# Last head of a retention layer: another order of its output tiles, and its first-freed tiles in a pool of their own

## The chip, the core and the metric

The kernel runs on one core of a Trainium2 chip. A core has a matrix engine (TensorE, PE in the profile, with its weight loads as PEld), a vector engine (VectorE, DVE), an activation engine (ScalarE, ACT), a general engine (GpSimd, POOL) and a queue engine that mostly issues DMAs (SyncE, SP). They run at the same time and wait for each other through semaphores; each works off its own instructions in the order in which they were placed. Operands lie in SBUF (128 partitions), matmul results in PSUM, eight banks of 128 x 512 fp32.

The metric is the time of one execution in microseconds of device time. A profiled execution gives the trace; its times are counted from the start of its span.

## The reference

One inference step of a two-layer decoder, on 512 prompt tokens and 32 sample tokens (8 sequences of 4) with shared weights. In what follows the 544 columns T are these tokens, prompt first.

```python
for i in range(DEPTH):            # layer 0: gated short convolution, layer 1: retention
    x = x + mixer(rmsnorm(x, norm_mix[i]))
    x = x + swiglu(rmsnorm(x, norm_ffn[i]))      # d_ff 2816
return rmsnorm(x, final_norm), conv states, retention states

def retention_mixer(x, s0, pos, w_in, gn_g, w_out):      # 4 heads, dk 256, dv 512
    q, k, v, g = split(x @ w_in)
    q, k = rotary(q, pos), rotary(k, pos) / 16
    o, S = retention_chunkwise(q, k, v, s0)      # decayed scores @ v + q @ state
    o = (o - mean(o)) * rsqrt(var(o) + 1e-6) * gn_g      # per head
    return (silu(g) * o) @ w_out, S
```

The sample tokens read and update a state of 256 x 512 per head and sequence; the prompt's state is an output. Everything is fp32.

## The kernel before

**Products.** Each fp32 operand is split into a high part (rounded, written by ScalarE) and a low part (the difference, by VectorE): `split`, L187. A product is three matmuls: high-high, high-low, low-high (`project`, L165, for 272 columns at a time; `mm3`, L160). The features lie on partitions, so `x` is 8 tiles of 128 x 544. Weights come by DMA into three rotating buffers `w` and are split into three rotating pairs `wh`, `wl`, all of one pool for the whole kernel. For three output-projection weight tiles of the last head the low part comes from ScalarE and a DMA that adds (`split_adding`, L192).

**Stages.** Convolution layer, first feed-forward, retention layer, second feed-forward, final norm. Each feed-forward (`ffn`, L545) works in 2 x 2 blocks with seven products in place of eight: VectorE and ScalarE form sums of weight blocks (`weights7`, L424) and of activation blocks (`operands_left`, `operands_rest`, L403 and L408). `run` (L511) goes through 22 jobs, gate and up by turns; a job's products come in the order 1, 5, 6, 2, 7, 4, 3 for the first one, and the weights of the next are prepared ahead. `gate` (L591) applies Silu. Product 1 and 5 need only the first four `x` tiles, the others all eight.

**Retention, head by head** (L1166). Values and keys; gate tiles 0 to 3 (`gate_project`, L994: matmuls, times the norm's factor, Silu, gain); scores; then the output by token tiles of 128: `inner(h, st, it)` (L1042), 9 matmuls of 512 columns for tile 2, 12 for tile 3; `sample_outputs` (L1100) and `states_update` (L1113) for the four parts of the samples' state, whose load (`states_load`, L1095) takes the buffer that an earlier part's store frees. `normalized` (L1030) takes mean and variance on VectorE, the power on POOL, and scales. `gated` (L1059) transposes a normalized tile on TensorE (4 transposes) and multiplies it with the gate on VectorE. `out_project` (L1132) splits the gated tiles (`yh`, `yl`) and adds eight output tiles to `x`, two to each weight tile, in the order 0, 1, 4, 5, 2, 3, 6, 7. The last head has no next head's work to overlap, so its gate tiles 2 and 3 are kept back to cover its waits, and the first weight tile's two outputs are done by halves of 272 columns: the first half needs token tiles 0, 1 and a part of 2, the second the rest.

**What sets the order.** A planner goes through the program once with estimated durations. On each engine it places next the instruction that comes first in the program among those that it reckons to be ready; a later one can fill a gap. So an instruction's place in the program is its rank, not its time. `issue_after` pins an instruction behind another. The engines then run that fixed order, and wait where the estimate was too early.

**Memory.** Pools lie in SBUF as a stack, in the order in which they are opened; a stage's pools take the addresses of the stage before, and a tile waits for the old tiles that it covers. In the retention layer the stack is `vp` (17.4 KB to a partition: values, later `yh` and `yl`), `tp` (tiles in the order of first use: `gt`, `rot0`, `rot1`, `rt0`, `rt1`, the split keys and queries, ...), `one`, `sp` (three state buffers). The second feed-forward stacks its gate and up tiles (17.4 KB) and then `sw` (18.4 KB), where the sums of weight blocks are made and split. So `sw` covers `gt`, `rot0`, `rot1`, `rt0`, `rt1` and a part of the keys. In the last head `gt` and `rot1` hold normalized tiles (L1216, L1224) and `rot0` one part of the prompt's mid state.

**PSUM.** Two double banks (`psum()`) and four single banks (`bank()`).

## Time and profile before

| | us |
|---|---|
| median of three runs (lowest, highest) | 1467.85 (1467.62, 1469.62) |
| the profiled execution | 1468.62 |
| its span, first to last instruction | 1466.4 |
| TensorE busy | 1449.5 (99%) |
| VectorE, ScalarE, POOL busy | 959.4, 632.1, 130.5 |
| DMA | 189.62 MB, mean 129 GB/s |

In the trace the last head's gate tiles 2 and 3 run from 1031.6 to 1046.2 us, its first output matmul stands at 1052.8, the last at 1080.0, and the second feed-forward's first product follows at 1080.1.

How to read the rows. A row of the timeline gives start, duration, engine, line, instruction, output<-inputs, a count where equal rows were merged, and in brackets the idle time before it and what ended it. Durations of neighbours on one engine overlap by some 0.1 us, so that start to start is shorter. A row of the windows gives, for a stretch, the busy time of each engine with the number of instructions, the TensorE clock granted (1.00 is full), the DMA share and GB/s. A row of the waits names who waited for whom. Tile names have lost their numbers: `h` and `l` are the split weight sums, `oh` and `ol` the split activation blocks, `f` the blocks before the split.

### The profile page before, as it was taken

How to read it: one execution, taken by the hardware profiler on the slowest of the kernel's cores; microseconds unless marked ns; L12 is line 12 of the kernel's file. 1: busy time of each engine (PE TensorE's matmuls, PEld its weight loads, DVE VectorE, ACT ScalarE, POOL GpSimd, SP SyncE). 2: the span in 40 equal slices, each digit the busy share in tenths (PEclk: the TensorE clock that was granted, in tenths of full speed). 3: DMA queues.
4: the chain of work that ended last, by engine and by line, in shares of the span. 5: the costliest groups of instructions: out<-in, count | busy, mean ns of one | idle time of the engine just before them, and what ended most of it. 6: DMA issues, size and time to landing. Idle time of an engine off the chain costs nothing.

```text
span 1466.4 us, 26224 instructions
## 1 busy us (share of the span) xinstructions
PE 1449.5 (99%) x10920; PEld 1378.7 (94%) x10920; DVE 959.4 (65%) x1489; ACT 632.1 (43%) x925; POOL 130.5 (9%) x171
## 2 busy tenths in 40 slices
PE   9999999999999999999999999999999999999997
PEld 9999999999999999898988978987789999999997
DVE  5644678848748557648546835835698847748655
ACT  5222467626536435241141223214286626526434
POOL 0100011101101003000000000000111101101002
PEclk9999999999999999999999999999999999999999
DMA  6222246635536436237234623713646635536432
GB/s 225 78 95 89 89 104 146 153 109 130 130 108 149 125 73 199 92 115 258 75 124 164 202 81 112 253 53 120 202 113 140 146 115 129 143 106 140 122 80 83
DMA packets 80694, 189.62 MB, mean 129 GB/s; under 512 B 7728, under 2 KB 25008, under 8 KB 80576
## 3 DMA queue, kind: packets, MB, share of 16 engines
q1 hardware_dynamic: 66576, 162.01, 35.2%
q0 software_dynamic: 13136, 24.72, 10.3%
q8 instruction: 85, 1.39, 0.4%
q10 hardware_dynamic: 864, 1.22, 0.2%
q14 instruction: 33, 0.27, 0.1%
HBM read 166.75 MB, written 21.18 MB: 128 GB/s over the span
## 4 chain that ended last, share of the span: by engine, by line
PE 90%; DVE 6%; DMA 1%; ACT 1%; POOL 1%; issue 1%; DVEq 0%; POOLq 0%; ACTq 0%
PE mm L173 37%; PE sm L476 31%; PE sm L173 8%; PE sm L897 2%; PE sm L898 2%; PE sm L899 2%; PE sm L161 1%; PE sm L163 1%; PE sm L162 1%; PE sm L1108 1%; DVE S L1129 1%; DMA w<-in_ffgu_dram 1%; DVE ol L189 1%; DVE wl L189 1%; DMA S<-in_rets_dram 1%
## 5 line engine op out<-in xcount | busy, mean ns | idle before, releaser
L188 ACT ACTIVATE wh<-w 128x1024 fp32r<-128x1024 f32 (+4 forms) x139 | 129.6, 936 | 346.6 <-PE mm L173 223.3
L476 PE MATMUL sm<-oh,wh 128*128 128x272 f32 x704 | 204.2, 290 | 3.1 <-ACT oh L188 1.7
L476 PE MATMUL sm<-ol,wh 128*128 128x272 f32 x704 | 203.5, 289 | 1.1 <-DVE ol L189 1.1
L476 PE MATMUL sm<-oh,wl 128*128 128x272 f32 x704 | 203.3, 289 | 0.2 <-DVE wl L420 0.2
L173 PE MATMUL mm<-xh,wh 128*128 128x272 f32 x932 | 195.3, 290 | 0.0
L173 PE MATMUL mm<-xh,wl 128*128 128x272 f32 x932 | 192.5, 289 | 0.0
L173 PE MATMUL mm<-xl,wh 128*128 128x272 f32 x932 | 192.4, 288 | 0.0
L189 DVE TENSOR_TENSOR wl<-w,wh 128x1024 fp32r<-128x1024 f32 (+4 forms) x139 | 150.2, 1085 | 27.7 <-ACT wh L188 25.4
L269 DVE TENSOR_TENSOR x<-x,mm 128x544 f32<-128x544 f32 x91 | 65.4, 719 | 139.1 <-PE mm L173 139.0
L476 PE MATMUL sm<-oh,h 128*128 128x272 f32 x528 | 152.0, 288 | 0.0
L476 PE MATMUL sm<-oh,l 128*128 128x272 f32 x528 | 151.7, 288 | 0.0
L476 PE MATMUL sm<-ol,h 128*128 128x272 f32 x528 | 151.6, 287 | 0.0
L173 PEld LDWEIGHTS mm<-xh,wh 128*128 128x128 f32 x932 | 146.5, 189 | 4.8 <-DVE wl L189 3.4
L173 PEld LDWEIGHTS mm<-xl,wh 128*128 128x128 f32 x932 | 146.2, 189 | 0.1
L173 PEld LDWEIGHTS mm<-xh,wl 128*128 128x128 f32 x932 | 145.5, 189 | 0.2
L476 PEld LDWEIGHTS sm<-oh,wh 128*128 128x128 f32 x704 | 132.7, 188 | 4.6 <-ACT oh L188 2.3
L476 PEld LDWEIGHTS sm<-ol,wh 128*128 128x128 f32 x704 | 132.8, 189 | 1.5 <-DVE ol L189 1.5
L476 PEld LDWEIGHTS sm<-oh,wl 128*128 128x128 f32 x704 | 133.5, 190 | 0.5 <-DVE wl L420 0.5
L422 POOL DMA_DIRECT2D wl<-in_ffgu_dram x88 | 75.5, 858 | 647.9 <-ACT wl L421 298.3
L419 ACT ACTIVATE wh<-w 128x1024 fp32r<-128x1024 f32 x88 | 93.3, 1060 | 75.0 <-PE sm L476 47.9
L476 PEld LDWEIGHTS sm<-oh,h 128*128 128x128 f32 x528 | 99.4, 188 | 0.2 <-ACT oh L188 0.2
L476 PEld LDWEIGHTS sm<-oh,l 128*128 128x128 f32 x528 | 99.6, 189 | 0.0
(260 smaller groups left out, 3087.3 us busy)
## 6 DMA issues: line engine op xcount, KB each, us to landing
w<-in_ffgu_dram SPq DMA_DIRECT2D x88, 512.0 KB, 4.0
wl<-in_ffgu_dram POOLq DMA_DIRECT2D x88, 256.0 KB, 4.7
w<-in_ffdn_dram SPq DMA_DIRECT2D x96, 192.0 KB, 2.6
S<-in_rets_dram SPq DMA_DIRECT2D x16, 1024.0 KB, 7.6
out_rets_dram<-S SPq DMA_DIRECT2D x16, 1024.0 KB, 5.5
w<-in_cvin_dram SPq DMA_DIRECT2D x21, 512.0 KB, 3.5
w<-in_rtqk_dram SPq DMA_DIRECT2D x16, 512.0 KB, 3.6
w<-in_rtv_dram SPq DMA_DIRECT2D x16, 512.0 KB, 3.6
```

Of the source, the lines that this page charges most:

```text
L161: nc.tensor.matmul(out, lh, rh, start=start, stop=False, skip_group_check=True)
L162: nc.tensor.matmul(out, lh, rl, start=False, stop=False, skip_group_check=True)
L173: last_product[0] = nc.tensor.matmul(half(pt, hf)[:, :HT], w[:, c], act[k][:, hf * HT : (hf + 1) * HT], start=(first and k == ks[0] and i ...
L188: h = nc.scalar.activation(dh, src, AF.Copy)
L189: last_low[0] = nc.vector.tensor_sub(dl, src, dh.bitcast(F32))
L269: last_residual[0] = nc.vector.tensor_add(xk, xk, p)
L419: nc.scalar.activation(wh, w, AF.Copy)
L422: nc.gpsimd.dma_start(wl[:, n:], src[:, n:], accum_op=ALU.add)
L476: last = nc.tensor.matmul(out, w[:, c], b[k][:, at, :], start=(first and k == 0 and i == 0), stop=(k == n - 1 and i == 2), skip_group_chec ...
L897: nc.tensor.matmul(out, xh[kt][:, ts_], wh[:, cw], start=(kt == 0), stop=False)
L898: nc.tensor.matmul(out, xh[kt][:, ts_], wl[:, cw], start=False, stop=False)
L899: nc.tensor.matmul(out, xl[kt][:, ts_], wh[:, cw], start=False, stop=(kt == KT - 1))
```

## The change

Five edits; the numbers of matmuls stay, as do the shapes, but for three output tiles.

1. The one-element activation at the start that makes ScalarE load a function table is a Silu, not a Copy.
2. The last head's order: token tile 2's `inner` moves from ahead of gate tiles 2 and 3 to behind them, next to tile 3's. The normalized rows of tile 2 and of the samples go into a state buffer (`free`), not into `gt` and `rot1`.
3. `out_project` of the last head does output tiles 0, 1 and 4 by parts: the first 256 columns (token tiles 0 and 1) for all three, then `rest()`, which transposes and gates the samples, tile 2 and tile 3, then the other 288 columns. Each part is added to `x` by itself. The third tile's parts lie in two single banks.
4. `gt`, `rot1`, `rt1` and the split keys move to a pool `ep` between `vp` and `tp`, 19.1 KB to a partition, which is where the feed-forward's `sw` comes to lie.
5. The first job's weights are prepared (`jobs[0].prepare()`) before the activation blocks are made, no longer after.

```diff
-                nc.scalar.activation(warm, ones[:, 0:1], AF.Copy)
+                nc.scalar.activation(warm, ones[:, 0:1], AF.Silu)
...
     def run(jobs, after, steps):
 
         jobs[0].lead = True
-        jobs[0].prepare()
         jobs[0].begin()
...
             wide("m")
+            jobs = [job for m in range(HJ) for job in gate_up(m)]
+            jobs[0].prepare()
             made = None
             for kt in PAIRED[layer]:
                 made = operand(kt)
...
         vp = c2.enter_context(tc.tile_pool(name="rtv", bufs=1, reuse_waits="tile"))
+
+        ep = c2.enter_context(tc.tile_pool(name="rte", bufs=1, reuse_waits="tile"))
         tp = c2.enter_context(tc.tile_pool(name="rt", bufs=2, reuse_waits="tile"))
...
-            gt = tp.tile([P, 2, T], F32, tag="gt", name=nm("gt"), bufs=1)
+            gt = ep.tile([P, 2, T], F32, tag="gt", name=nm("gt"), bufs=1)
...
-                tp.tile([P, 2, T], F32, tag=f"rot{w}", name=nm("rot"), bufs=1) for w in range(2)
+                pool.tile([P, 2, T], F32, tag=f"rot{w}", name=nm("rot"), bufs=1) for w, pool in enumerate((tp, ep))
...
-            t1 = tp.tile([P, T], F32, tag="rt1", name=nm("rt1"), bufs=1)
+            t1 = ep.tile([P, T], F32, tag="rt1", name=nm("rt1"), bufs=1)
...
+            pool = ep if which else tp
+            th = pool.tile([P, 2, SEQ], F32R, tag=f"qkh{which}", name=nm("qkh"), bufs=1)
+            tl = pool.tile([P, 2, SEQ], F32R, tag=f"qkl{which}", name=nm("qkl"), bufs=1)
...
-        def normalized(src, tag="yn"):
+        def normalized(src, yn=None):
...
-            split_gated(slice(0, HT if rest else T))
-            wide("m" if rest else "mms")
-            for n2 in (0, 2, 1, 3):
-                wh, wl = load_piece(a["rtout"][h, n2], 2 * 4 * P, adding=rest is not None and n2 > 0)
-                pts = []
-                for n in range(2):
-                    pts.append(psum())
-                    if n2 == 0 and rest:
-                        rest[n]()
-                        project(pts[n], wh, wl, n * 4 * P, yh, yl, hfs=(0,))
-                    else:
-                        project(pts[n], wh, wl, n * 4 * P, yh, yl)
-                        residual(2 * n2 + n, pts[n])
-                if n2 == 0 and rest:
-                    split_gated(slice(HT, T))
-                    for n in range(2):
-                        project(pts[n], wh, wl, n * 4 * P, yh, yl, hfs=(1,))
-                        residual(n, pts[n])
+            cut = 2 * P
+            def part(pt, w, n, c):
+
+                for k in range(4):
+                    at = slice((n % 2 * 4 + k) * P, (n % 2 * 4 + k + 1) * P)
+                    mm3(
+                        pt[:, : c.stop - c.start], w[0][:, at], w[1][:, at], yh[k][:, c], yl[k][:, c], k == 0, k == 3
+                    )
+
+            order = (0, 1, 4, 5, 2, 3, 6, 7)
+            ws, parts = {}, {}
+            split_gated(slice(0, cut if rest else T))
+            wide("m" if rest else "mms")
+            for i, n in enumerate(order):
+                if i % 2 == 0:
+                    ws[n // 2] = load_piece(a["rtout"][h, n // 2], 2 * 4 * P, adding=rest is not None and n > 0)
+                if rest and i < 3:
+                    parts[n] = psum() if i < 2 else [bank(), bank()]
+                    part(half(parts[n], 0), ws[n // 2], n, slice(0, cut))
+                    if i == 2:
+                        rest()
+                        split_gated(slice(cut, T))
+                        for m, pt in parts.items():
+                            part(half(pt, 1), ws[m // 2], m, slice(cut, T))
+                            for c, b in ((slice(0, cut), 0), (slice(cut, T), 1)):
+                                nc.vector.tensor_add(x[m][:, c], x[m][:, c], half(pt, b)[:, : c.stop - c.start])
+                    continue
+                pt = psum()
+                project(pt, *ws[n // 2], n % 2 * 4 * P, yh, yl)
+                residual(n, pt)
...
             sample_outputs(h, st, 2)
-            p2 = inner(h, st, 2)
             if more:
+                p2 = inner(h, st, 2)
                 nxt = qk_start(h + 1)
...
             else:
-                yn2 = normalized(p2, "gt")
                 gate_project(h, st, 2, lambda: states_update(h, st, 2))
...
                 gate_project(h, st, 3, inside)
-                yns = normalized(st["po"], "rot1")
                 gated_pair(h, st, (yn0, 0), (yn1, 1))
-                gated(h, st, yn2, 2)
-                p3 = inner(h, st, 3)
-                gated(h, st, yns, 4)
+                p2, p3 = inner(h, st, 2), inner(h, st, 3)
+                free = sp.tile([P, 4, DV], F32, tag="S", name=nm("yn"))
+                yns, yn2 = normalized(st["po"], free[:, 0, :]), normalized(p2, free[:, 1, :])
                 yn3 = normalized(p3)
-                out_project(h, st, [lambda: None, lambda: gated(h, st, yn3, 3)])
+
+                def rest():
+                    gated(h, st, yns, 4)
+                    gated(h, st, yn2, 2)
+                    gated(h, st, yn3, 3)
+
+                out_project(h, st, rest)
```

The tiles `v4` (tag `rot1`) and one of `v2` (tag `rt1`) move to `ep` with their tags, in the same way.

10 lines of the change are left out of this document (4 added, 6 removed).

## The prediction

> **What bounds the kernel.** I read the page's busy shares first, then who TensorE waited for, then single stretches. The page:
>
> ```profile
> PE 1449.5 (99%) x10920; PEld 1378.7 (94%) x10920; DVE 959.4 (65%) x1489; ACT 632.1 (43%) x925; POOL 130.5 (9%) x171
> ```
>
> TensorE is busy 99% of the span and no matmul is removed, so only its waits and its slow stretches can be won. All its waits from 1046 to 1100 us (the last head and the start of the second feed-forward), then two from the list for the whole span (columns: us in total, times, longest):
>
> ```profile
> PE sm L476 <- ACT oh L188: 1.7, 1, 1.7
> PE mm L173 <- ACT yh L188: 1.2, 1, 1.2
> PE sm L476 <- DVE ol L189: 0.8, 1, 0.8
> PE sm L161 <- DVE yn L1039: 0.4, 1, 0.4
> PE sm L1063 <- DVE yn L1039: 0.3, 1, 0.3
> PE sm L476 <- ACT g L536: 0.2, 1, 0.2
> PE sm L476 <- DVE wl L420: 0.2, 1, 0.2
> ...
> PE sm L476 <- ACT u L536: 0.8, 1, 0.8
> ...
> PE sm L173 <- DVE rs L222: 0.3, 1, 0.3
> ```
>
> Three sit at the feed-forward's start (oh 1.7, ol 0.8, wl 0.2: 2.7 us), four in the last head. Busy time by stretch (PE, PEld, DVE, ACT, POOL with instruction counts; PEclk; DMA):
>
> ```profile
> 1058.70:1080.10 21.40, 21.40 (x170) 21.17 (x170) 20.50 (x38) 19.39 (x31) 1.73 (x2) 1.00 0.31 62
> ...
> 1051.00:1054.40 3.40, 2.11 (x14) 1.47 (x12) 2.89 (x8) 1.39 (x4) 0.73 (x1) 1.00 0.80 155
> 1054.40:1057.80 3.40, 3.22 (x15) 3.22 (x16) 1.43 (x5) 0.00 (x0) 0.00 (x0) 0.52 0.20 39
> ...
> 1081.70:1085.10 3.40, 0.84 (x4) 0.41 (x4) 3.40 (x8) 2.11 (x4) 0.00 (x0) 1.00 0.00 0
> 1085.10:1088.50 3.40, 3.18 (x13) 2.91 (x14) 3.40 (x6) 1.72 (x4) 0.85 (x1) 0.53 0.46 118
> ...
> 1065.00:1088.70 23.70, 20.80 (x150) 19.88 (x149) 23.41 (x42) 20.73 (x33) 2.59 (x3) 0.93 0.33 72
> ```
>
> A 272-column matmul takes 21.40/170 = 0.126 us. A stretch in which TensorE idled is twice followed by 3.4 us at a granted clock of 0.52 and 0.53: half of 3.22 and of 3.18 us, 1.6 us lost each time. So the losses that the change can touch are: 0.8 (L536, in the first feed-forward) + 0.3 (gate tile 2) + 0.4 + 1.2 + 0.3 (output projection's start) + 1.6 + 2.7 + 1.6 + 0.2 = **9.1 us**. From 1065 on VectorE is busy 23.41 of 23.70 us: it, not TensorE, sets when the last operands of the second feed-forward exist.
>
> **The change, part by part.**
>
> *Silu in the warm-up.*
>
> ```profile
> 221.41 1.28 ACT L598 ACT_TABLE_LOAD   x1
> ...
> 225.34 0.38 ACT L536 ACTIVATE u<-sm 128x272 f32<-128x272 f32 x1
> ...
> 225.77 0.39 PE L476 MATMUL sm<-oh,wh 128*128 128x272 f32 x1 [0.84 <-ACT u L536]
> ```
>
> The load in front of the first Silu goes; the one at the warm-up stays, in time that waits for the first DMA anyway. ScalarE's queue behind it comes 1.28 us earlier, more than the 0.84 that TensorE waited for the snapshot. Bounds 0 and 0.8; I take 0.8, as ScalarE ran without a gap from the load to that snapshot.
>
> *Output tile 2 moved behind the gate tiles.* Its nine 512-column matmuls change place, not number. Its PSUM bank is no longer held while gate tile 2 asks for two, so that wait (0.3) goes. Both gate tiles come earlier by 0.3 and by the nine matmuls; but with them comes the last state's product (L1108), which needs a state from memory:
>
> ```profile
> 1050.11 0.40 PE L162 MATMUL sm<-vl,sh 128*128 128x512 f32 x1
> 1050.34 0.39 PE L163 MATMUL sm<-vh,sl 128*128 128x512 f32 x1
> ...
> 1031.91 1.51 SPq L1098 DMA_DIRECT2D S<-in_rets_dram  x1
> ...
> S<-in_rets_dram SPq DMA_DIRECT2D x1, 1024.0 KB, 8.6
> ...
> 1041.72 1.04 PE L1108 MATMUL sm<-S,qm 128*8 128x512 f32 x8
> ...
> 800.46 1.05 PE L1108 MATMUL sm<-S,qm 128*8 128x512 f32 x8 [0.24 <-DMA S<-in_rets_dram]
> ```
>
> Nine matmuls of 0.23 are 2.1 us, so the product is reached at 1041.72 - 2.4 = 1039.3, while the state lands at 1031.91 + 8.6 = 1040.5. Nothing moves the load: SP issues it behind the second state's store, as before. That is a new wait of 1.2 us; head 1 shows the same wait, 0.24, at a margin that the planner had thought enough. Bounds 0 (the planner puts the rest of gate tile 3 in front) and 1.2; I take 1.2, by the load's own row. Behind it on TensorE stand the last state update and half of gate tile 3, whose end I call E: 1046.2 - 2.4 + 1.2 = 1045.0.
>
> *From E to the first output matmul.*
>
> ```profile
> 1047.55 0.78 DVE L1006 TENSOR_TENSOR gate<-sm,R 128x272 f32<-128x272 f32 x2
> 1049.84 0.69 DVE L1066 TENSOR_TENSOR gate<-gate,mm 128x512 f32<-128x512 f32 x1 [1.51 <-ACT gate L1008]
> 1051.04 0.69 DVE L1035 BATCH_NORM_STATS2 bst<-sm 128x6 f32<-128x512 f32 x1
> 1053.71 0.81 DVE L1039 TENSOR_SCALAR yn<-sm,mv,rs 128x512 f32<-128x512 f32 x1 [0.46 <-POOL rs L223]
> ```
>
> From the gate's first multiplication to the end of the pair's gating is 1051.0 - 1047.55 = 3.5 us (two rows of 0.6 net each at its end). After E that is E + 0.4 + 3.5, and the first split is done near E + 4.4. TensorE has meanwhile 8 transposes (0.9), tile 2 (2.1) and tile 3 (12 x 0.23 = 2.8): until E + 5.8. The 1.2 and the 0.4 are covered. What is late next is tile 3's normalization: 1054.5 - 1051.0 = 3.5 us on VectorE and POOL, so E + 5.8 + 0.3 + 3.5 = E + 9.6. The three 256-column parts (36 x 0.126 x 256/272 = 4.3 us) cover it to E + 10.1. The 0.3 goes too, with half a microsecond to spare. The tile that now holds the normalized rows takes the second state's buffer, whose store is issued ahead of the load at 1031.91: free long before E.
>
> *The end of `rest`.* Its 12 transposes (1.3 us) now stand together, and nothing else on TensorE is ready behind them: all further output matmuls need the 288 columns that are gated and split last.
>
> ```profile
> 1057.55 0.69 DVE L1066 TENSOR_TENSOR gate<-gate,sm 128x512 f32<-128x512 f32 x1 [1.97 <-PE sm L1063]
> 1058.27 1.39 ACT L188 ACTIVATE yh<-gate 128x272 fp32r<-128x272 f32 x4 [4.53 <-DVE gate L1066]
> ...
> 1058.75 0.52 PE L173 MATMUL mm<-yh,wh 128*128 128x272 f32 x2
> ```
>
> Last transpose to gating, split and matmul took 1.2 us there, under other matmuls; in the new order it lies open. Bounds 0 (the planner puts the transposes among the parts) and 1.2; I take 1.2. With it may come a half-clock stretch as after 1051-1054.4, where PE's rows cover 2.11 of 3.40 us: bounds 0 and 1.6; the new gap is as long as the old one, but how it falls into the clock's stretches isn't known, so I take 0.8. The second parts, 36 x 0.133 = 4.8 us, and five whole tiles, 120 x 0.126 = 15.1, then run without a gap: T + 19.9, T being their start, E + 12.6.
>
> *Weights first, in memory that is free early.* The rows of the first job's weights on VectorE:
>
> ```profile
> 1047.28 0.35 SPq L431 DMA_DIRECT2D w<-in_ffgu_dram  x1
> ...
> 1060.14 0.68 DVE L434 TENSOR_TENSOR w<-w 128x512 f32<-128x512 f32 x1
> ...
> 1085.03 0.68 DVE L420 TENSOR_TENSOR wl<-w,wh 128x512 fp32r<-128x512 f32 x1
> 1085.64 1.00 DVE L189 TENSOR_TENSOR ol<-f,oh 128x816 fp32r<-128x816 f32 x1
> ...
> 1086.91 1.21 DVE L189 TENSOR_TENSOR l<-w,h 128x1024 fp32r<-128x1024 f32 x1
> 1088.04 0.72 DVE L189 TENSOR_TENSOR ol<-f,oh 128x544 fp32r<-128x544 f32 x1
> ```
>
> Four sums (L434 to L437, 0.6 net each: 2.4) and two low parts (1.1 + 0.6) no longer need memory that the normalized tiles hold, and the later of the two loads that they read is issued at 1047.28: 4.1 us can go into VectorE's gap from E + 9.6 to E + 11.6 and the smaller gaps about it. What remains after T: 23.41 - 1.7 (L420, L189 `l`) = 21.7 us of operands, sums of squares and residuals, 1.7 of the same that ran before 1065, two L420 (1.2), and 0.3 for the residuals in two pieces: 24.9. From the first residual at T + 1.9, less the last square (0.6), the last operand stands at T + 26.2. TensorE can do products 1 and 5 and the first three blocks of one or two more without it, 33 to 42 matmuls: to T + 24.1 or 25.2. Stall 1.0 to 2.1; I take 1.5, and no half clock, in place of 2.7 + 1.6. Bounds: 0, and 5.6 if the 4.1 us stay where they are. The second job's weights follow the operands on ScalarE and VectorE and are needed 60 matmuls (7.6 us) after T + 19.9: in time, barely. SP's order of loads is untouched; POOL gets the same three powers, later. The 0.2 at L536 stays.
>
> **Sum.** 9.1 lost before; after 1.2 + 1.2 + 0.8 + 1.5 + 0.2 = 4.9; gain 4.2 us. The profiled execution took 1468.62 us (span 1466.4 and 2.2 around it) and would take 1464.4; it stands 0.8 above the median of the runs, 1467.85, so the forecast is **1463.6 us**.
>
> **Rivals.**
> - *No half clock.* The remaining idle pieces are too short: 0.8 less, 1462.8. For it: none of the new gaps is longer than 1.5 us. Against it: the gap of 1.2 before 1054.4 was enough. The Trainium skill ("TensorE: Matmul & The Clock Gate", Part 1) says that the clock halves after an idle window of about 3.4 us, and its closing table warns of gaps over some 3 us; by that rule this rival holds. The trace disagrees: 1.2 us of waiting, with PE's rows covering 2.11 of 3.40 us, was followed by a clock of 0.52.
> - *VectorE stays the bound.* The sums and low parts find no gap before T: 4.1 us come back, 1467.7, no change that can be told. For it: VectorE was idle before 1057.55 with L434's load landed, and L434 still came at 1060.14. Against: its memory was then the normalized tiles'.
> - *Slower: ScalarE blocks on the weights.* Now written ahead of the operands, `weights7`'s first rounding (L419) needs the `wh` buffer that the second output weight tile gives back when output tiles 4 and 5 are done, T + 4.8 + 3.0 = T + 7.8. If it stands in ScalarE's queue ahead of the first operand scaling (L580), ready at T + 2.0, all operands slip 5.8 us, and the longer stall adds a half-clock stretch, 1.6: 1463.6 + 7.4 = 1471.0. It decides as soon as L419 precedes the third L580. Against it, the rows of before, where it was placed at the buffer's release:
>
> ```profile
> 1061.66 0.75 ACT L580 ACTIVATE f<-x,vec 128x544 f32<-128x544 f32 x1 [2.01 <-DVE x L269]
> ...
> 1069.02 1.05 ACT L419 ACTIVATE wh<-w 128x1024 fp32r<-128x1024 f32 x1
> ```
>
> **How the numbers follow.** The measurement tells 0.2%, 2.9 us, from no change. Forecast 0.52, its own range 1459.2 (all goes but the 0.2 and one small wait) to 1464.9; no half clock 0.12; VectorE the bound 0.20; ScalarE blocked 0.12; 0.04 for an order that the planner changes elsewhere, on the slow side. Faster 0.64, within 0.2% 0.20, slower 0.16. The range takes in all but the outer part of the blocked case: 1459.0 to 1470.5.
>
> **What would show it.** Right: one table load; no wait of gate tile 2; L1108 of the last head waiting about 1 us for its state; no gap before the first `yh` matmul; one gap of about 1.2 after the last transposes; L434 before T; the wait for `oh` and `ol` at L476 under 2 us. Wrong: L434 still after the splits, L419 ahead of the L580s, two half-clock stretches, or a new wait over 1 us anywhere between 230 and 1030 us.

## The result, and the profile after

The changed kernel takes 1473.2 us (median; 1472.22 to 1473.75) against 1467.85 for the kernel before, measured beside it: a ratio of 1.0032, with a 95% interval of 1.0021 to 1.0044. It is slower by some 5 us, where 4.2 us of gain were forecast. The profiled execution has a span of 1470.3 us, 3.9 more than before. The page of the changed kernel, busy times:

```profile
PE 1450.5 (99%) x10920; PEld 1379.5 (94%) x10920; DVE 959.7 (65%) x1492; ACT 631.3 (43%) x924; POOL 130.9 (9%) x171
```

The work is the same; only waits and slow stretches can differ. Where TensorE waited in the changed kernel between 1032 and 1102 us (total, times, longest):

```profile
PE mm L161 <- ACT yh L188: 2.6, 2, 1.4
PE sm L476 <- ACT oh L188: 1.6, 2, 1.3
PE sm L476 <- DVE wl L420: 1.3, 1, 1.3
PE sm L476 <- DVE ol L189: 1.1, 2, 0.7
PE sm L1112 <- DMA S<-in_rets_dram: 0.5, 1, 0.5
PE mm L162 <- DVE yl L189: 0.2, 1, 0.2
```

The last head's waits (`yh`, S, `yl`) sum to 3.3 us and those at the feed-forward's start (`oh`, `wl`, `ol`) to 4.0, where before had 2.7. The same kernel by stretches of 3.41 us (busy time of PE, PEld, DVE, ACT, POOL; clock granted to TensorE; DMA):

```profile
1083.46:1086.87 3.41, 1.46 (x8) 1.01 (x8) 3.41 (x8) 3.41 (x7) 0.00 (x0) 0.99 0.00 0
1086.87:1090.28 3.41, 3.41 (x15) 3.41 (x15) 3.41 (x7) 1.65 (x3) 0.85 (x1) 0.51 0.35 40
1090.28:1093.70 3.42, 1.66 (x10) 1.15 (x9) 3.42 (x5) 2.90 (x4) 0.47 (x1) 0.99 0.24 42
1093.70:1097.11 3.41, 3.41 (x17) 3.41 (x17) 1.70 (x4) 0.00 (x0) 0.39 (x1) 0.50 0.87 215
1097.11:1100.52 3.41, 3.41 (x18) 3.41 (x17) 1.71 (x4) 0.79 (x2) 1.57 (x1) 0.51 0.52 169
```

Three of the five stretches have the clock at half: 5.1 us lost (half of 10.24), where before had one such stretch at this place (1.7 us). Two follow directly on a stretch with 1.8 to 2.0 us of waits. The third follows a stretch in which TensorE did not wait at all; what that stretch holds comes up below.

The last head's output ends 0.4 us earlier than before (first matmul of the feed-forward behind it: 1079.7 against 1080.1). The spread of the norm's factor, L227, comes at 1102.22 against 1098.28, 3.9 us later, and this is the whole difference of the spans. So, on balance, everything is lost in the 22 us in which the second feed-forward starts.

What VectorE did there (start, duration, idle time before in brackets):

```profile
1061.93 0.79 DVE L1172 TENSOR_TENSOR x<-x,mm 128x256 f32<-128x256 f32 x2 [0.71 <-PE mm L163]
1063.39 0.79 DVE L1172 TENSOR_TENSOR x<-x,mm 128x256 f32<-128x256 f32 x2 [0.67 <-PE mm L163]
...
1064.85 0.45 DVE L1172 TENSOR_TENSOR x<-x,sm 128x288 f32<-128x288 f32 x1 [0.32 <-PE sm L163]
1066.53 0.73 DVE L189 TENSOR_TENSOR ol<-f,oh 128x544 fp32r<-128x544 f32 x1 [1.22 <-ACT oh L188]
...
1070.23 0.68 DVE L434 TENSOR_TENSOR w<-w 128x512 f32<-128x512 f32 x1
...
1088.96 0.68 DVE L435 TENSOR_TENSOR w<-w,w 128x512 f32<-128x512 f32 x1
1089.57 0.68 DVE L436 TENSOR_TENSOR w<-w,w 128x512 f32<-128x512 f32 x1
1090.17 0.71 DVE L189 TENSOR_TENSOR ol<-f,oh 128x544 fp32r<-128x544 f32 x1
```

It stood still for 2.9 us at the beginning, and L434, L435 and L436 in these rows are sums for the *second* job: the first job's were done by 1059 us. The last operand's low part, `ol`, comes at 1090.17 (before: 1088.04). ScalarE, in the same kernel:

```profile
1063.41 1.05 ACT L194 ACTIVATE wh<-w 128x1024 fp32r<-128x1024 f32 x1
...
1064.91 1.04 ACT L195 ACTIVATE wl<-wh 128x1024 fp32r<-128x1024 f32 x1
1065.86 0.64 ACT L188 ACTIVATE oh<-f 128x544 fp32r<-128x544 f32 x1
...
1067.61 1.06 ACT L419 ACTIVATE wh<-w 128x1024 fp32r<-128x1024 f32 x1
...
1090.32 1.06 ACT L419 ACTIVATE wh<-w 128x1024 fp32r<-128x1024 f32 x1
1091.36 1.06 ACT L188 ACTIVATE h<-w 128x1024 fp32r<-128x1024 f32 x1
1092.32 0.61 ACT L421 ACTIVATE wl<-wh 128x512 fp32r<-128x512 f32 x1
1092.84 0.38 ACT L535 ACTIVATE g<-sm 128x272 f32<-128x272 f32 x1
```

The first job's weights (L419 at 1067.61) stand among the operands, and from 1090.32 three roundings for the second job stand in front of the first job's own snapshot (L535). In before the snapshot came ahead of all of them:

```profile
1088.44 0.40 ACT L536 ACTIVATE g<-sm 128x272 f32<-128x272 f32 x1 [0.22 <-PE sm L476]
```

The loads of the second job's weights, of which L430 is issued first and L431 second, in before and then in the changed kernel:

```profile
1063.39 0.35 SPq L430 DMA_DIRECT2D w<-in_ffgu_dram  x1
1085.79 0.33 SPq L431 DMA_DIRECT2D w<-in_ffgu_dram  x1
```

```profile
1064.48 0.35 SPq L430 DMA_DIRECT2D w<-in_ffgu_dram  x1
1069.70 0.33 SPq L431 DMA_DIRECT2D w<-in_ffgu_dram  x1
```

The second load follows at once on the end of a low part of the first job (L420), the last instruction to read its `w` buffer on VectorE: 1085.71 in before, 1069.67 now. So it is issued 16 us earlier, and the second job's weights are at hand too soon.

**A second measure.** Each execution comes with its mean granted clock. One minus it, times the span, is what the half clock cost if TensorE was busy meanwhile: on average 8.8 us in the changed kernel and 5.1 in before (some of it at the very end of the kernel, in both). What is left of the span, 1462.0 against about 1461, is the time without clock losses. The clock is recorded in steps of 0.001, which are 1.5 us of a span, so only means over several executions are used here, and differences of a few tenths of a microsecond say nothing. So about 3.7 of the 5 us are clock and 1 to 1.4 are waits. The experiments give both numbers: "clock" is this loss, "rest" the remaining span. Their ratios are to the kernel before, run beside each, which took 1467.8 to 1468.8 us.

### The profile page after: what moved, and what is told of

Read it like the earlier page. It is cut to its first block, busy times and chain, and to the rows that moved or that the text cites. A ratio compares the mean times of both kernels' runs of the same rounds, so it can differ in the third digit from the quotient of the medians.

```text
span 1470.3 us, 26228 instructions
## 1 busy us (share of the span) xinstructions
PE 1450.5 (99%) x10920; PEld 1379.5 (94%) x10920; DVE 959.7 (65%) x1492; ACT 631.3 (43%) x924; POOL 130.9 (9%) x171
## 4 chain that ended last, share of the span: by engine, by line
PE 88%; DVE 6%; DMA 3%; ACT 1%; POOL 1%; issue 1%; SPq 0%; DVEq 0%; POOLq 0%; ACTq 0%
PE mm L173 35%; PE sm L476 31%; PE sm L173 7%; PE sm L900 2%; PE sm L901 2%; PE sm L902 2%; DMA S<-in_rets_dram 2%; PE sm L161 1%; PE sm L163 1%; PE sm L162 1%; DVE S L1133 1%; DMA w<-in_ffgu_dram 1%; PE sm L1112 1%; DVE ol L189 1%; DVE wl L189 1%; PE mm L907 1%
## 5 line engine op out<-in xcount | busy, mean ns | idle before, releaser
L419 ACT ACTIVATE wh<-w 128x1024 fp32r<-128x1024 f32 x88 | 93.3, 1060 | 73.1 <-PE sm L476 48.3
L476 PEld LDWEIGHTS sm<-ol,h 128*128 128x128 f32 x528 | 99.8, 189 | 0.7 <-DVE ol L189 0.7
```

What stands on the lines that cost most here:

```text
L419: nc.scalar.activation(wh, w, AF.Copy)
L476: last = nc.tensor.matmul(out, w[:, c], b[k][:, at, :], start=(first and k == 0 and i == 0), stop=(k == n - 1 and i == 2), skip_group_chec ...
```

## The experiments

### Which edit

Theory A: the weights that are now written ahead of the operands stand among them in the queues of VectorE and ScalarE. Theory B: the last head's new order makes the operands' inputs arrive in a worse sequence. First A's edit undone in the changed kernel (`a_prepback`), then done alone in before (`b_prep`):

```diff
         jobs[0].lead = True
+        jobs[0].prepare()
         jobs[0].begin()
...
             jobs = [job for m in range(HJ) for job in gate_up(m)]
-            jobs[0].prepare()
```

> The changed kernel, with the first job's weights prepared behind the activation blocks again, as before the change; its other four edits stay. Theory A (rank): written ahead of the blocks, the weight work stands among the blocks in the queues of VectorE and ScalarE, which are what TensorE waits for at the feed-forward's start, and the last block comes later (1090.9 instead of 1088.7). Then this kernel wins back about 4 us of the changed kernel's 1473.2: 1468 to 1469.5, one or two half-clock stretches. Theory B (arrival): the three output tiles by parts bring the first residuals late (1062 to 1065 us), and the blocks start late whatever the weights do: 1472.5 to 1473.5, unchanged.

Measured: 1469.58 us, 1.0004 of before [0.9995, 1.0013]; clock 5.6, rest 1461.9.

> The kernel before, with nothing but the first job's weights prepared ahead of the activation blocks. Theory A: slower by 2 to 5 us, 1470 to 1473, with the waits for oh, ol and wl at L476 longer than 2.7 us in all. Theory B: 1467 to 1468.5, no change.

Measured: 1474.19 us, 1.0029 [1.0020, 1.0038]; clock 7.4, rest 1463.7 (before in the same session 5.1 and 1461.5). In its profile the waits for `oh`, `ol` and `wl` come to 3.7 us in place of 2.7, and four stretches on end, 13.7 us, are at half clock.

Before with the new order, its three cut tiles and the normalized rows in the state buffer only (`ep = tp`, Copy in the warm-up, `prepare` behind the operands), and before with Silu only:

```diff
-        ep = c2.enter_context(tc.tile_pool(name="rte", bufs=1, reuse_waits="tile"))
         tp = c2.enter_context(tc.tile_pool(name="rt", bufs=2, reuse_waits="tile"))
+        ep = tp
```

> The kernel before, with nothing but the last head's own order, the three output tiles by 256 and 288 columns, and the normalized rows in a state buffer. Theory A: the last head's small gain alone (its last output matmul came 0.4 us earlier in the changed kernel), 1466.5 to 1468. Theory B: the loss is here, 1471 to 1473.

Measured: 1470.92 us, 1.0014 [1.0005, 1.0022]; clock 6.0, rest 1462.5.

```diff
-                nc.scalar.activation(warm, ones[:, 0:1], AF.Copy)
+                nc.scalar.activation(warm, ones[:, 0:1], AF.Silu)
```

> The kernel before, with nothing but Silu in the warm-up activation. Both theories: one table load less, TensorE's wait of 0.84 us at 225 us gone, 1466.8 to 1467.3; any more or less comes from the planner's order elsewhere.

Measured: 1467.78 us, 0.9993 [0.9984, 1.0002].

Reading: the weights put first cost 0.28 to 0.29%, whether taken out or put in; the new order costs 0.14% by itself; Silu gains about 0.07%, within what can be told from nothing. 0.29 + 0.14 - 0.07 = 0.36 against the measured 0.32. Theory A holds for the larger part, and the order, which was to bring the gain, brings a loss. The new pool alone was not run.

### Whose weights

In the changed kernel the second job's preparation is pinned behind the last operand's split; the first job's stays first:

```diff
             if nxt is not None:
-                nxt.prepare()
+                with ExitStack() as behind:
+                    if i == 0:
+                        for p in pins:        # last operand's split, both engines
+                            behind.enter_context(tc.issue_after(p))
+                    nxt.prepare()
```

> After, with one thing undone in part: the second feed-forward's second job (of 22) has its weights prepared only behind the last operand's split on ScalarE and VectorE; the first job's stay ahead of the operands. In after the second job's L434 (1070.23), two more sums (1088.96, 1089.57) and one ScalarE rounding (L419, 1081.00) stand between the operands' instructions. Theory 'the second job's weights are among the operands': about 2 us of VectorE and 1 us of ScalarE leave the operands' way, the last low part `ol` comes some 2 us earlier than 1090.17, and a half-clock stretch of 3.4 us (1.7 us) goes: 1469 to 1471 us, ratio 0.997 to 0.999 against after, 1.001 to 1.002 against before. Rival 'the first job's own L419 and L420 are the cost': nothing changes, 1472 to 1474; the second job's weights, now late, may even add a wait at L476 on `wl` of 1 to 2 us.

Measured: 1471.25 us, 1.0023 [1.0014, 1.0032]; clock 7.1, rest 1461.8. The waits at the start fall from 4.0 to 3.0 us, but only 1.3 us of time come back (by the ratios), and the interval overlaps that of the changed kernel: less than expected, and a half-clock stretch was not saved (three in its profile, as in the changed kernel's).

Only the loads and the four sums first, the rounding and the low parts back behind the operands:

```diff
         nc.vector.tensor_sub(w4, a12, s2)
+        return lambda: split7(src1, src2, sw, w1, w2, w3, w4)
...
-            jobs[0].prepare()
+            jobs[0].sums()
             made = None
```

> After, with the first job's preparation cut in two: the loads and the four sums (L434 to L437, 2.4 us of VectorE) stay ahead of the operands in rank, the rounding and the low parts (ScalarE's L419, L188 and L421, VectorE's L420 and L189) go back behind them, as in before. Theory 'the sums go into VectorE's gaps for nothing, and what hurts is the rounding among the operands': at least as fast as with the whole preparation put back (1.0004 of before): 1466 to 1469 us, ratio 0.998 to 1.000, last low part `ol` before 1088. Rival 'any weight work ahead of the operands hurts': between that and after, 1470 to 1473.

Measured: 1468.55 us, 1.0008 [0.9999, 1.0017]; clock 5.3, rest 1461.5. So sums in VectorE's gaps do no harm that can be measured, and gain nothing: the harm comes with the rounding and the low parts among the operands. What is moved back here also holds the `w` buffer longer (the second job's second load is issued at 1090.77 in this profile), so this run does not tell the first job's own rounding from the early weights of the second job. The run before it puts the second job's share at 0.09 of the 0.28%.

### Is the clock the cost, or the waits?

In the changed kernel, three unread 128-column matmuls on a tile of ones behind each product block of the first job:

```diff
+                if self.lead and self.fill:
+                    with tc.issue_after(last.ins):
+                        for _ in range(self.fill):
+                            last = nc.tensor.matmul(self.pad[:, 0, :P], ones, ones, start=True, stop=True)
```

> After, with matmuls added that compute nothing used: behind each product block of the second feed-forward's first job three 128-column matmuls on a tile of ones (some 70 in all, about 0.06 us each at full clock), which keep TensorE busy where it waits for operands. Theory 'what is lost is mostly the half clock that follows idle pieces' (10.2 us at half clock in after, 5.1 us of loss): the half-clock stretches at the feed-forward's start shrink by one or two (1.7 to 3.4 us), against up to 4 us of added work of which about half stands in waits: 1470 to 1473 us. Rival 'what is lost is the idle time itself': nothing is gained and the added work is paid in part: 1474 to 1477 us.

Measured: 1481.53 us, 1.0093 [1.0079, 1.0107]. The added work was much larger than estimated: 84 matmuls that the trace shows as two instructions each, 168 of 0.104 us, 17.5 us. But the clock loss falls to 3.0 us, and the stretch has no wait left and a full clock:

```profile
1081.30:1111.30 30.00, 30.00 (x258) 29.92 (x257) 18.55 (x33) 14.59 (x24) 3.39 (x4) 1.00 0.26 59
```

The account closes within 1 us: 1462.0 (rest of the changed kernel) - 4.0 (waits now filled) + 17.5 = 1475.5, against a measured rest of 1476.5. By time both named outcomes were missed; by the clock the first is right.

Next, the stretch without waits that is followed by another at half clock. In 1093.7 to 1097.1 TensorE spends 0.84 us (three pairs of 0.28, start to start) in L247, matmuls of one column that make the norm's sums. In the changed kernel they and the spread of the factor are moved some 80 matmuls later (the first tiles' gate is then scaled with the factor of the stage before):

```diff
-                if which not in (5, 6, 2):
+                if which not in (5, 6, 2, 1 if lateweave[0] else 5):
...
-        jobs[0].weave = jobs[1].weave = steps
+        jobs[0].weave = iter(()) if lateweave[0] else steps
+        jobs[1].weave = steps
```

> After, with the ten one-column matmuls of the second feed-forward's norm (L247) and the spread of its factor (L227) moved some 80 matmuls (10 us) later, out of the first job and behind the disturbed stretch; the matmuls before that point keep their order. Theory 'the one-column matmuls count as idle for the clock': in after the second half-clock stretch at that place (1097.1 to 1100.5) follows one (1093.7 to 1097.1) in which TensorE never waits, but spends 0.84 us in L247; without them this stretch is granted the full clock: 1.7 us less, 1470.5 to 1472.5 us, some 5.1 us of half clock behind 1086 where after had 10.2 fall to 6.8. Rival 'the clock follows the waits alone, with a delay': 10.2 us at half clock stay, and the time stays at 1472 to 1474.

Measured: 1471.15 us, 1.0022 [1.0013, 1.0031]; clock 6.6, rest 1462.4: 2.2 us less clock loss than the changed kernel, at the same waits within 0.4 us. A cleaner form, in the kernel with the second job pinned: four of the five pairs go a dozen matmuls further on, and no other instruction of any engine changes place.

```diff
-                if which not in (5, 6, 2):
+                if which not in (5, 6, 2, 7 if self.lead and lateweave[0] else 5):
...
-            steps = rms_scale(rest=9)
+            lateweave[0] = bool(layer)
+            steps = rms_scale(rest=5 if layer else 9)
```

> The kernel with the second job's weights pinned behind the operands, with the five pairs of one-column matmuls (L247) some twelve matmuls further on, out of the half-clock stretches at 1088.5 to 1095.3, and no other instruction changed on any engine. In that kernel the waits end at 1088.9, yet the clock stays halved until 1098.7, over two stretches with 0.6 and 1.1 us of L247. Theory 'one-column matmuls count as idle, and at half clock they last twice as long': one or two of the three stretches go, 1.7 to 3.4 us less: 1468 to 1469.7 us, ratio to before 1.000 to 1.0012, lost to the clock about 4 to 5.5 us in place of 7.1. Rival 'three stretches follow from the waits alone': 1471 to 1472, ratio 1.0015 to 1.003, lost 7 us as before.

Measured: 1468.09 us, 1.0002 [0.9993, 1.0011], 0.21% less than without the move; clock 4.5, rest 1461.6. First the windows of the kernel with the second job pinned, then those of this one:

```profile
1085.10:1088.50 3.40, 1.81 (x8) 0.97 (x7) 3.11 (x7) 2.03 (x3) 0.00 (x0) 1.00 0.02 5
1088.50:1091.90 3.40, 3.22 (x14) 3.23 (x15) 3.40 (x7) 2.46 (x5) 0.85 (x1) 0.51 0.18 24
1091.90:1095.30 3.40, 3.40 (x18) 3.40 (x17) 2.59 (x5) 1.38 (x3) 0.55 (x1) 0.50 0.93 211
1095.30:1098.70 3.40, 3.40 (x17) 3.40 (x17) 1.29 (x2) 0.40 (x1) 1.53 (x2) 0.50 0.84 222
```

```profile
1085.10:1088.50 3.40, 1.58 (x6) 0.95 (x6) 3.11 (x6) 1.98 (x4) 0.00 (x0) 1.00 0.02 5
1088.50:1091.90 3.40, 3.03 (x22) 2.82 (x23) 3.40 (x7) 2.46 (x4) 0.85 (x1) 1.00 0.00 0
1091.90:1095.30 3.40, 3.40 (x30) 3.40 (x30) 3.21 (x6) 2.26 (x5) 1.13 (x2) 1.00 0.95 210
1095.30:1098.70 3.40, 3.37 (x28) 3.16 (x28) 1.90 (x4) 2.33 (x4) 0.95 (x1) 1.00 0.88 214
```

The waits are the same in both (3.0 us), the instructions too. The rest is equal within 0.2 us, and the mean clock loss falls from 7.1 to 4.5 over all executions, which is what the time shows. These two profiles differ by more than the move: even the first stretch behind the waits kept its full clock in the second. The borders of the stretches can be continued from the half-clock stretch that each trace has near the kernel's end, 3.413 us at a time. In the first kernel they put 0.72, 1.63 and 0.14 us of TensorE's idle time into three stretches in turn, in the second 0.71, 1.20 and 1.11, so that no stretch of the second has as much as halves the clock elsewhere. Its profile therefore says nothing of the move; the means over eleven executions do.

### Can the waits be moved?

One wait looked needless: in the changed kernel TensorE waits 1.32 us for the second job's low weights (L420) while the first job's product 7 seems ready behind it. The second job's first product was pinned behind product 7; only seven matmuls change place:

```diff
             if nxt is not None:
-                nxt.begin()
+                with tc.issue_after(seven[0].ins) if seven[1] and i == 0 else ExitStack():
+                    nxt.begin()
```

> After, with the second feed-forward's second job's first product pinned behind the first job's product 7: seven matmuls on TensorE change place (in after three of them stand among the first job's), nothing on VectorE, ScalarE or SP. Theory 'a wait for the second job's weights in front of ready work': the wait of 1.32 us for L420's `wl` at 1091.45 goes, the stretch in which it lies is left with 0.44 us of waits, and the two half-clock stretches behind it (1093.7 to 1100.5, 3.4 us) go: up to 4.7 us less than after, 1468.5 to 1470 us, ratio to before 1.000 to 1.0015; lost to the clock about 5.5 us in place of 8.8. Rival 'the operands are late whatever TensorE does first': the wait comes back at another matmul, 1472 to 1474 us.

Measured: 1474.4 us, 1.0041 [1.0028, 1.0053]; clock 9.7, rest 1462.7. The theory fell. TensorE's waits at the start:

```profile
PE sm L476 <- ACT g L539: 1.7, 1, 1.7
PE sm L476 <- ACT oh L188: 1.7, 2, 1.4
PE sm L476 <- DVE ol L189: 0.9, 2, 0.6
```

Product 7 was not ready: it goes into the accumulator whose snapshot (L539 here, L535 above) stood in ScalarE's queue behind the second job's three roundings. The wait changed its name and grew by 0.4 us.

The wait ahead of the first output matmul: tile 2's normalization pinned behind the gating of tile 1, so that VectorE does not stand for POOL's power in front of it:

```diff
-                yns, yn2 = normalized(st["po"], free[:, 0, :]), normalized(p2, free[:, 1, :])
+                yns = normalized(st["po"], free[:, 0, :])
+                with tc.issue_after(last_gating[0].ins):
+                    yn2 = normalized(p2, free[:, 1, :])
```

> After, with the normalization of token tile 2 pinned behind the gating of token tile 1, so that VectorE does not stand for POOL's power (0.76 us) in front of the gating that the first split waits for. Theory 'the order on VectorE makes the wait of 1.14 us in front of the first output matmul': it falls to 0.1 to 0.5 us, the operands start that much earlier: 1472 to 1473 us where after had 1473.2, that is 0.3 to 1.0 us less, as far as the rest of the start is unchanged. Rival 'the wait is gate tile 3's own length': it stays above 0.9 us. In both cases the loss at the feed-forward's start stays.

Measured: 1475.32 us, 1.0054 [1.0040, 1.0067]; clock 11.5, rest 1461.5. The cause of the wait was right (1.14 falls to 0.51), but tile 2 is late in turn: the second wait grows from 1.43 to 1.91, and two of 0.25 for `yl` stand where there was one of 0.2. The rest is 0.5 us below the changed kernel's; the time is 2 us above it, all of it clock.

### Is VectorE the bound?

The sums of squares of the second feed-forward's norm, six VectorE instructions, go to POOL, in the changed kernel (`a_sqpool`) and in before with Silu (`s_sqpool`):

```diff
-                    square_sum(kt, None, add=nc.vector)
+                    square_sum(kt, None, add=None if layer else nc.vector)
```

> After, with the sums of squares of the second feed-forward's norm added up on POOL in place of VectorE: six VectorE instructions of about 0.64 us leave the stretch in which the operands are made (3.8 us); POOL takes them at about 1.4 to 1.8 us each, on nobody's way but the norm's. Theory 'VectorE's queue sets when the operands exist': the last low part `ol` comes 2 to 4 us earlier than 1090.17, and the idle pieces and half-clock stretches at the start shrink: 1468 to 1471 us. Rival 'ScalarE or the loads set it': within 1 us of after, 1472 to 1474.

Measured: 1475.37 us, 1.0046 [1.0033, 1.0058]; clock 8.0, rest 1464.9.

> Before, with the first of the five edits alone (Silu in the warm-up) and the same move of the sums of squares to POOL. Theory 'VectorE's queue sets when the operands exist': before's three waits at the feed-forward's start (1.7, 0.8, 0.2 us) and one half-clock stretch (1.6 us) shrink by 2 to 4 us, and Silu gives up to 0.9: 1464 to 1466 us, ratio 0.997 to 0.999. Rival 'ScalarE or the loads set it': as Silu alone, 1467 to 1468, ratio 0.999 to 1.000.

Measured: 1468.13 us, 1.0000 [0.9991, 1.0009]; clock 2.8, rest 1463.5. Of the time that was hoped for nothing came; the ratio is the rival's, but not for the rival's reason: there is less clock loss and more of everything else. POOL's and VectorE's rows in the second kernel:

```profile
1068.85 2.22 POOL L218 TENSOR_TENSOR sqacc<-sqacc,sqlast 128x544 f32<-128x544 f32 x1 [1.84 <-ACT sqlast L217]
1071.85 1.36 POOL L218 TENSOR_TENSOR sqacc<-sqacc,sqlast 128x544 f32<-128x544 f32 x1 [0.77 <-ACT sqlast L217]
```

```profile
1067.23 0.43 DVE L411 TENSOR_TENSOR f<-f 128x272 f32<-128x272 f32 x1
...
1069.77 1.60 DVE L413 TENSOR_TENSOR f<-f 128x272 f32<-128x272 f32 x1
1071.29 0.68 DVE L420 TENSOR_TENSOR wl<-w,wh 128x512 fp32r<-128x512 f32 x1
1071.89 1.61 DVE L410 TENSOR_TENSOR f<-f 128x272 f32<-128x272 f32 x1
```

A VectorE subtraction of two SBUF operands takes 0.43 us alone and 1.6 while POOL adds, and it ends 0.3 us after POOL's addition (1071.37 and 1071.07, 1073.50 and 1073.21). What left VectorE's queue came back as standing time, and the residuals behind it made the output projection wait. The Trainium skill ("SBUF — State Buffer", the section on the two separate sides) says that VectorE and GpSimd share a pair of ports as an exclusive lock, not as a share of bandwidth; this trace agrees (0.43 against 1.60 us). So whether VectorE's load is the bound stays open by this way; that the *order* of the weight work among the operands matters was shown above.

### Versions of the kernel before without the half clock

Before with Silu and unread matmuls in its waits. All have five ahead of the last head's first output matmul, and `s_gap1` only these. `s_fill` has ten more behind the second and third block of product 1; there the planner's order puts them behind the waits, where they are mere work. `s_fill2` has its ten inside product 2, where TensorE stands:

```diff
                         rest[n]()
+                        if n == 0:
+                            with tc.issue_after(last_product[0].ins):
+                                for _ in range(5):
+                                    nc.tensor.matmul(pts[0][:, 0, :P], ones, ones, start=True, stop=True)
                         project(pts[n], wh, wl, n * 4 * P, yh, yl, hfs=(0,))
...
+                    if filled[0] and self.lead and which == 2 and (k, i) in ((1, 0), (2, 2)):
+                        with tc.issue_after(last.ins):
+                            for _ in range(3 if k == 1 else 7):
+                                nc.tensor.matmul(filled[0][:, 0, :P], ones, ones, start=True, stop=True)
```

> Before, with Silu in the warm-up and 15 added matmuls on a tile of ones (128 columns in two passes, about 0.21 us each) whose results nobody reads: 5 in front of the last head's first output matmul (wait 1.2 us), 3 and 7 in front of the second feed-forward's third and fourth block (waits 0.8 and 1.7 us). Theory 'those waits cost their length and, each, a half-clock stretch of 3.4 us': nearly all of the added 3.1 us lies in waits, and the half-clock stretches (one or two in before, 1.7 us each) go: 1464.5 to 1466.5 us, ratio 0.998 to 0.999. Rival 'the half clock is not set by these waits': the stretches stay and the time is that of Silu alone or above, 1467.5 to 1469, ratio 0.999 to 1.001.

Measured: 1469.15 us, 1.0011 [1.0002, 1.0020]; clock 4.8, rest 1462.2.

> Before, with Silu in the warm-up and 5 unread matmuls on a tile of ones (two passes of 0.1 us each, 1.1 to 1.3 us in all) in the wait of 1.2 us ahead of the last head's first output matmul, and nowhere else. Theory 'that wait costs its length and then a half-clock stretch': the stretch (1.7 us) goes where it occurred, and the added work lies in the wait: 1465.5 to 1467.5 us, ratio 0.998 to 0.9995, against 0.9993 with Silu alone. Rival 'no stretch hangs on it': 1467.5 to 1468.5.

Measured: 1467.97 us, 0.9993 [0.9984, 1.0002]; clock 4.7, rest 1461.1: as with Silu alone.

> As the run with one filled wait, and with 3 more unread matmuls in the wait of 0.8 us and 7 in that of 1.7 us at the second feed-forward's start, inside product 2, where TensorE stands. Theory 'the waits' half-clock stretches are what can be saved without touching the operands': TensorE is busy through the waits, no half-clock stretch between 1050 and 1100, about 3.4 us less lost to the clock than in before: 1463.5 to 1466 us, ratio 0.997 to 0.9985. Rival: the fill delays the matmuls behind it by as much as the clock gains, 1466.5 to 1468.5.

Measured: 1467.12 us, 0.9995 [0.9986, 1.0003]; clock 3.2, rest 1462.1. No stretch between 1030 and 1115 us is at half clock in its profile, as expected, but half of the 1.9 us won comes back in the rest. TensorE now runs into the operands' next instructions:

```profile
PE sm L476 <- DVE l L189: 0.6, 1, 0.6
PE sm L476 <- DVE ol L189: 0.5, 1, 0.5
PE sm L476 <- ACT g L541: 0.4, 1, 0.4
```

Two kernels take what was learned: before with Silu, the first job's weights first, the second's pinned and the one-column matmuls moved, but the old order and memory of the last head (`c_noorder`: the edits of `b_silu`, `b_prep`, `a_second` and `c_norm` in one); and the same with the five unread matmuls of `s_gap1` (`c_gap1`).

> Before with Silu, the first job's weights ahead of the operands, the second job's pinned behind them and the norm's one-column matmuls some twelve matmuls later; the last head's order, its output parts and its memory as in before. Theory 'the parts add up': the kernel with the new order as well came out at 1.0002, and the new order alone costs 0.14%, so this one lies at 0.998 to 0.9995: 1465 to 1467 us where before has 1467.9. Rival 'without the new pool the weight sums stay behind the normalized tiles and nothing is won': 0.9995 to 1.001, 1467 to 1469.5.

Measured: 1467.34 us, 0.9995 [0.9986, 1.0004]; clock 4.0, rest 1461.3 (before beside it: 5.2 and 1460.7).

> The same, with the five unread matmuls on a tile of ones in the 1.2 us wait ahead of the last head's first output matmul, and no other change of order. Theory 'a half-clock stretch hangs on that wait in part of the executions': 0.3 to 1.5 us less than without them, 1464 to 1466.5 us, ratio 0.9975 to 0.999. Rival: no difference within 0.3 us.

Measured: 1468.09 us, 0.9999 [0.9990, 1.0008]; clock 4.5, rest 1461.1: the five matmuls gain nothing on top.

The parts add up to within 0.1% (1.0002 - 0.0014 = 0.9988 expected, 0.9995 measured), and no version is told apart from before. Where clock losses are saved, the rest grows (by 0.6 us here, 0.8 in `s_fill2`); why is not shown in each case, but in `s_fill2` the new waits are for the operands' chain on VectorE and ScalarE.

## Why the prediction was wrong, step by step

- **Silu.** Right: the wait for the snapshot `u` is gone, and the table load with it. Not foreseen: the weights first also act in the *first* feed-forward, where the wait for `ol` goes from 0.26 to 0.73 us (0.7 with the weights first alone, 0.2 with Silu alone). The step was priced for the second feed-forward alone.
- **Gate tile 2's bank.** Right, the wait is gone.
- **The last state's load.** The mechanism is right; the size was 0.49 us in this execution in place of 1.2. In profiles of kernels with the same order it lies between 0.1 and 1.7 us, so the term is a spread, not a number.
- **"The 1.2 and the 0.4 are covered."** Half wrong: the 0.4 is gone, but 1.14 us stand in front of the first output matmul. The chain of 4.4 us was taken from rows in which VectorE had nothing else to do. Its second part, the gating of token tile 1, now stands behind tile 2's statistics and POOL's power. The five rows are from VectorE and ScalarE of the changed kernel; the run with tile 2 pinned confirms it.

```profile
1048.81 0.15 DVE L222 TENSOR_SCALAR rs<-mv 128x1 f32<-128x1 f32 x1
1049.72 0.81 DVE L1043 TENSOR_SCALAR yn<-sm,mv,rs 128x512 f32<-128x512 f32 x1 [0.76 <-POOL rs L223]
1050.45 0.68 DVE L1070 TENSOR_TENSOR gate<-gate,mm 128x512 f32<-128x512 f32 x1
```

```profile
1047.21 0.75 ACT L1011 ACTIVATE gate<-gate,vec 128x544 f32<-128x544 f32 x1
1051.22 1.34 ACT L188 ACTIVATE yh<-gate 128x256 fp32r<-128x256 f32 x4 [3.26 <-DVE gate L1070]
```

- **The gap behind the last transposes.** Right: 1.43 us for 1.2, and in this execution no half-clock stretch follows (0.8 was taken, between 0 and 1.6).
- **Sums before T.** Right, and worth nothing: L434 to L437 and both low parts were done by 1059.8, as forecast but for the last 0.4; with the sums alone kept ahead, no gain could be measured.
- **The start of the second feed-forward, the step that failed.** "The last operand stands at T + 26.2 ... I take 1.5, and no half clock." It stood at T + 31.5 (T is 1059.35, the end 1090.88). The budget of 24.9 us counted VectorE's work and took it to be unbroken. VectorE idled 2.9 us at its beginning, behind residuals in two pieces and behind ScalarE's output weights (L194, L195); and 1.8 us of sums for the second job stood ahead of the last operand. 26.2 + 2.9 + 1.8 = 30.9; the other 0.6 stay unaccounted for. The step "the second job's weights follow the operands" was wrong for both engines: an instruction's rank is not its place, and the buffer for their second load came free 16 us earlier. The stall was 4.0 us in place of 1.5.
- **No half clock.** It came three times, 5.1 us. This is the largest term and was put at 0.8 for the whole change. The prediction asked whether *a gap* was long enough; what counted was the sum of the pieces within a stretch, and behind a halved stretch the one-column matmuls too.
- **The sum.** With what this execution shows, the prediction's terms are 0.5 (the state's load) + 1.1 (first output matmul) + 1.6 (behind the transposes) + 4.0 + 5.1 = 12.3 us, where 4.9 were forecast and 9.1 lost before. These 3.2 us and the 0.5 in the first feed-forward are 3.7 of the 3.9 us by which the span grew.
- **Rivals.** "Slower: ScalarE blocks on the weights" had the right engine and side, and its sign came true: L419 does precede the third scaling. But ScalarE did not block (L419 at 1067.61 started without idle time): it cost its 1 us each time, not 5.8. "VectorE stays the bound" did not come about by its mechanism, since the sums and low parts did find their gaps, and its time, 1467.7, lacked the clock. "No half clock" (1462.8) is refuted.

## What to carry to other kernels

Before work is moved ahead of a critical chain, count what *its* early end sets free: buffers, then loads, then the next stage's work, which lands in the same queues in front of the chain. Pin that work, or move only the part that fits into gaps that the trace shows (here the sums, not the rounding). And price waits on a matmul engine by stretches of the clock: several short waits can cost half of the 3.4 us that follow, and behind a halved stretch still shorter ones, or matmuls that stream almost nothing, prolong it.

## What the runs showed of the hardware

- The half clock comes in stretches of 3.41 us or several on end (1086.87 to 1090.28, 1093.70 to 1100.52). Within a trace their borders lie on one grid, which begins elsewhere in each trace: in the changed kernel's one halved stretch begins at 1086.82 and another, near the kernel's end, at 1465.70, 111 times 3.413 us later. The Trainium skill ("TensorE: Matmul & The Clock Gate", Part 1) gives a free-running window of 3413 ns, which agrees; its closing table's advice, no idle gaps over some 3 us between bursts, was not enough here, where the longest gap in front of a halved stretch was 1.73 in before and 1.32 in the changed kernel.
- What counts is TensorE's idle time within such a stretch. Counted on each trace's own grid from 1030 to 1115 us (all 20 traces), all 15 stretches at full clock with 1.70 us or more of it were followed by a halved one, none with 1.44 or less, and 11 of 14 between 1.45 and 1.68. In the changed kernel 1.99 and 1.76 us were made up of pieces of 0.25 to 1.32; a single wait of 1.43 had no halved stretch behind it.
- Behind a halved stretch less is enough. On the same count, halved stretches without one-column matmuls were followed by full clock with up to 0.38 us of idle time, and by another halved one with 0.58 or more. Without idle time, up to two pairs of one-column matmuls were followed by full clock (3 of 3), three or four pairs by another halved stretch (6 of 6). A pair takes 0.28 us at half clock and 0.14 at full clock, start to start; at full clock all five pairs within one stretch had full clock behind them (before and two others). So these matmuls prolong a halved clock here, and were not seen to halve one. Moving them took 2.2 and 2.6 us off the mean clock loss, in two kernels.
- The same edit thus changes the clock more than the waits: tile 2 pinned has about 0.5 us less of the rest than the changed kernel and 2.7 more of the clock (five executions).
- VectorE's subtractions of two SBUF tensors (128x272) take up to 1.6 us in place of 0.43 while POOL adds two SBUF tensors (128x544).
